# Second FFN: eight chunks done whole as four pairs, the first weight tiles of a pair with seven block products

## The chip, the cores and the metric

The kernel runs on one core of a Trainium2 chip. The metric is device time in microseconds (us), as the median of several runs. Engines are named as in the profile: PE is TensorE (matrix products), PEld its loading of the stationary operand, DVE is VectorE, ACT is ScalarE, POOL is GpSimd, SP is SyncE, which issues the DMAs.

## The reference

The kernel computes one block on 256 tokens of width 2048, in float32: a first gated feed-forward layer (FFN), a mixer (differential attention on half of the width, a causal depthwise convolution on the other), and a second FFN, each with a residual sum. Each of the three is entered through an RMS norm whose result is scaled and shifted, and left through a gate; scales, shifts and gates come from a vector c.

```python
ada = silu(c) @ w_ada + b_ada                  # 9 vectors of 2048: shift, scale, gate, three times
h = rms_norm(x) * (1 + scale) + shift
x = x + 0.5 * gate * swiglu(h, w_gu, w_down)   # FFN, first and last
...
def swiglu(h, w_gu, w_down):                   # d_ff = 5632
    g, u = split(h @ w_gu)
    return (silu(g) * u) @ w_down
```

## The kernel before

**Precision.** TensorE multiplies in a reduced-width float32 (fp32r). So each operand is split in a high part (a cast on ScalarE) and a low part (the difference, on VectorE), and a product is three matmuls: high by high, high by low, low by high (`mm3`, lines 331, 335 and 336). The activations are the stationary operand (128 x 128), the weights the moving one (128 x 512).

**Weights.** `w_tile` (from line 290) loads a weight tile of 512 x 512 numbers (1 MB) through SyncE's queue into one of four buffers (`raw`), and splits it in two halves of 128 x 1024 per engine instruction: `whi` by ScalarE (line 307), `wlo` by VectorE (line 309). There are four buffers of each, so the halves are at most four at a time, one of them under TensorE. `mm_tile` (line 344) runs the 24 matmuls of a tile: four k, two halves of the tokens, three matmuls each, into two PSUM banks, and then a `tick`, which starts what was put off by some tiles with `after_tiles`. Six PSUM banks are in the pool `acc`, two in `tp`.

**Order.** A planner (the framework's) orders each engine's instructions ahead of time: by the order of the program text, by when operands and buffers come free in its own estimate of the times. On the chip each engine runs its list in order and waits at semaphores.

**The feed-forward layer** (`ffn`, line 664). The 11264 columns of w_gu are 22 chunks of 512 (256 gate columns, 256 up columns); the 2048 rows are four tiles (pc 0 to 3). For the second FFN:

1. The first stage (`stage_a`, line 686): for every chunk the product with the first tile (pc 0) alone, copied by ScalarE from the banks into a part buffer of the chunk (line 691). The rest of the normed activations is made meanwhile (`pieces`), as soon as its scales and shifts are there.
2. Chunks begun early (`early`, here 3, 4 and 5): the product with tile pc 1 is added to the part (line 811).
3. The main groups (line 892): chunks 0 to 2 together, then one chunk at a time, over the tiles that are left. `finish` (line 852) of a chunk comes after the first tile of the next: VectorE adds the banks to the part (855), ScalarE takes silu of the gate half (856), VectorE multiplies (857). The result is then transposed: it is a 4-byte number in two 2-byte planes (copy by ScalarE, 861), turned by a DMA transpose from SyncE's queue (876), put together again (ScalarE, 870) and split in high and low (352, 353). In the second FFN all chunks go this way, in the first FFN the odd ones; the even ones are transposed on TensorE (886).
4. The down projection (`down_strassen`, line 490): 22 tiles in each of two halves; seven of the 22 are done as a 2 x 2 block product with seven block products (Strassen's method in Winograd's form) in place of eight; the others plainly.

**Modulation rows.** `ada(j)` (line 189) computes 128 of the 9 x 2048 modulation numbers: a 1 MB DMA into a `raw` buffer and one multiply-and-sum against the broadcast c (`c_bc`) on VectorE (line 195), and for every second j an addition of the bias (199). There are 144; those of the second FFN are rows 96 to 143. They are dealt out among the weight tiles by shares: in the second FFN 0.6 a tile until row 128, and then 0.5 until row 144. `modulation` (line 230) forms 1 + scale, times the norm's weight, one k at a time (line 237).

**Buffers.** 28 buffers of 4 KB per partition (`blk`) hold the parts, the normed activations (eight) and the transposed results; six (`tmp`) of 2 KB hold temporaries. `c_bc` has one buffer of its own, which the down projection uses again once the rows are done.

## Time and profile before

| | |
|---|---|
| median of 3 runs | 1821.1 us (1820.06 to 1821.19) |
| the profiled execution | 1820.38 us, of which the span of the profile 1818.5 us |
| TensorE | busy 1790.5 us, 8033 matmuls |
| weight load (PEld) | busy 1475.1 us |
| VectorE | busy 1521.1 us |
| ScalarE | busy 1056.5 us |
| GpSimd | busy 29.2 us |
| DMA | 507.19 MB, mean 279 GB/s |

The span runs from the first instruction to the last. The busy time of an engine is the time in which at least one of its instructions runs. Matmuls overlap: each is shown with some 390 ns, though they start closer together, so what one takes is read from successive starts. The same holds for VectorE and ScalarE to a smaller extent. A group's row names the line, the engine, the operation, what is written and read, the count, the busy time and the mean duration in ns, and the engine's idle time before it with what ended that.

### The profile page before, as it was taken

To read this page: it belongs to the slowest core of one execution; us is meant where nothing else is said; L and a number is where in the kernel's file an instruction comes from. 1 tells how busy PE (TensorE), PEld (TensorE's weight loads), DVE (VectorE), ACT (ScalarE), POOL (GpSimd) and SP (SyncE) were. 2 spreads that over 40 slices of the span, in tenths; PEclk is the share of its full clock that TensorE was granted. 3 is DMA by queue.
4 is the path that set the end of the run, shared out by engine and by line. 5 is a ranking of instruction groups with operands and counts; after the bars stand their busy time and mean duration, and the time that the engine had idled before them with its cause. 6 is when DMAs were issued, how large, how long until landed. Compare 5 with 4: busy or idle time off the path is not lost.

```text
span 1818.5 us, 21751 instructions
## 1 busy us (share of the span) xinstructions
PE 1790.5 (98%) x8033; PEld 1475.1 (81%) x8033; DVE 1521.1 (84%) x2018; ACT 1056.5 (58%) x1563; POOL 29.2 (2%) x29
## 2 busy tenths in 40 slices
...
GB/s 378 357 307 313 354 338 295 351 318 331 334 339 373 331 335 344 275 257 205 182 143 163 175 330 276 324 329 313 281 304 310 316 222 205 212 199 219 199 216 107
DMA packets 118138, 507.19 MB, mean 279 GB/s; under 512 B 53600, under 2 KB 54032, under 8 KB 60560
## 3 DMA queue, kind: packets, MB, share of 16 engines
...
## 4 chain that ended last, share of the span: by engine, by line
PE 86%; DVE 8%; ACT 2%; DMA 2%; issue 2%; SPq 0%; POOLq 0%; POOL 0%; DVEq 0%; ACTq 0%
PE acc L335 27%; PE acc L336 27%; PE acc L331 27%; DVE wlo L309 2%; DVE raw L195 1%; PE tp L335 1%; ACT whi L307 1%; PE tp L336 1%; PE tp L331 1%; DMA blk<-in_w_gu_dram 1%; PE acc L1171 1%; DVE wlo L538 1%; DVE blk L1063 1%; DMA raw<-in_w_gu_dram 0%; DVE blk L309 0%
## 5 line engine op out<-in xcount | busy, mean ns | idle before, releaser
L335 PE MATMUL acc<-wlo,blk 128*128 128x512 f32 x2340 | 913.0, 390 | 8.4 <-DVE wlo L309 8.4
L331 PE MATMUL acc<-whi,blk 128*128 128x512 f32 x2343 | 910.3, 391 | 2.5 <-ACT blk L405 1.3
L336 PE MATMUL acc<-whi,blk 128*128 128x512 f32 x2340 | 912.0, 390 | 0.0
L309 DVE TENSOR_TENSOR wlo<-raw,whi 128x1024 fp32r<-128x1024 f32 (+1 forms) x581 | 692.5, 1211 | 187.8 <-ACT whi L307 186.8
L307 ACT CAST whi<-raw 128x1024 fp32r<-128x1024 f32 (+1 forms) x581 | 597.2, 1044 | 428.8 <-PE acc L336 285.7
L335 PEld LDWEIGHTS acc<-wlo,blk 128*128 128x128 f32 x2340 | 439.5, 188 | 103.9 <-DVE wlo L309 13.4
L331 PEld LDWEIGHTS acc<-whi,blk 128*128 128x128 f32 x2343 | 440.0, 188 | 94.5 <-ACT whi L307 2.0
L336 PEld LDWEIGHTS acc<-whi,blk 128*128 128x128 f32 x2340 | 439.3, 188 | 92.0 <-DVE blk L407 0.8
L195 DVE CUSTOM_DVE_ANT_0 raw<-raw,c_bc 128x2048 f32<-128x2048 f32 x142 | 324.2, 2285 | 4.9 <-DMA raw<-in_w_ada_dram 4.9
L537 ACT CAST whi<-raw 128x1024 fp32r<-128x1024 f32 (+1 forms) x56 | 53.0, 946 | 68.2 <-PE tp L336 31.9
L538 DVE TENSOR_TENSOR wlo<-raw,whi 128x1024 fp32r<-128x1024 f32 (+1 forms) x56 | 60.8, 1088 | 19.3 <-ACT whi L537 19.1
L1063 DVE SCALAR_TENSOR_TENSOR blk<-blk,cst,blk 128x247 f32<-128x247 f32 (+21 forms) x176 | 70.5, 460 | 0.0
L870 ACT COPY tmp<-tmp 128x1024 uint16<-128x1024 uint16 x33 | 44.9, 1359 | 37.7 <-DMA tmp<-tmp 37.6
L691 ACT COPY blk<-acc 128x512 f32<-128x512 f32 x72 | 41.6, 588 | 42.7 <-PE acc L336 40.7
L856 ACT ACTIVATE blk<-blk 128x256 f32<-128x256 f32 x88 | 34.9, 413 | 43.7 <-DVE blk L855 43.5
L855 DVE TENSOR_TENSOR blk<-acc,blk 128x512 f32<-128x512 f32 x88 | 57.2, 683 | 2.1 <-PE acc L336 2.1
L331 PE MATMUL acc<-blk,blk 128*128 128x512 f32 x104 | 40.7, 394 | 0.9 <-ACT blk L323 0.9
L861 ACT COPY tmp<-blk 128x1024 uint16<-128x1024 uint16 x33 | 34.4, 1043 | 10.4 <-DVE blk L857 10.2
L335 PE MATMUL acc<-blk,blk 128*128 128x512 f32 x100 | 39.1, 391 | 0.5 <-DVE blk L309 0.5
L336 PE MATMUL acc<-blk,blk 128*128 128x512 f32 x100 | 39.1, 392 | 0.0
L857 DVE TENSOR_TENSOR blk<-blk 128x256 f32<-128x256 f32 x88 | 34.9, 418 | 0.7 <-ACT blk L856 0.6
L353 DVE TENSOR_TENSOR blk<-tmp,blk 128x512 fp32r<-128x512 f32 x33 | 22.7, 688 | 14.4 <-ACT blk L352 14.4
...
## 6 DMA issues: line engine op xcount, KB each, us to landing
raw<-in_w_gu_dram SPq DMA_DIRECT2D x161, 1024.0 KB, 6.4
...
```

Source lines behind the costliest of these rows:

```text
L195: nc.vector.tensor_tensor_reduce(out=raw, in0=raw, in1=c_bc, scale=1.0, scalar=0.0, op0=ALU.mult, op1=ALU.add, accum_out=ada_cols[g][:, j ...
L307: nc.scalar.copy(out=hi[:, :m, :], in_=rw)
L309: nc.vector.tensor_sub(out=lo[:, :m, :], in0=rw, in1=hi[:, :m, :].bitcast(F32))
L331: nc.tensor.matmul(acc, ah, wh, start=start, stop=False)
L335: nc.tensor.matmul(acc, ah, wl, start=False, stop=False)
L336: return nc.tensor.matmul(acc, al, wh, start=False, stop=stop)
L537: nc.scalar.copy(out=hi[:, :n, :], in_=src)
L538: nc.vector.tensor_sub(out=lo[:, :n, :], in0=src, in1=hi[:, :n, :].bitcast(F32))
L691: last_part[0] = nc.scalar.copy(out=parts[c][:, t, :], in_=accs[t])
L855: nc.vector.tensor_add(out=p[:, t, :], in0=accs[t], in1=p[:, t, :])
L870: nc.scalar.copy(out=src.bitcast(U16).rearrange("p i t (s b) -> p b t i s", b=2), in_=turned)
L1063: nc.vector.scalar_tensor_tensor(out=y[:, d:], in0=u, scalar=w, in1=y[:, d:], op0=ALU.mult, op1=ALU.add)
```

## The change

In the second FFN the last eight chunks (14 to 21) are no longer done in the first stage. They are done whole, as four pairs, after chunk 12; chunk 13 comes last. Each pair begins with `pair_first`: the first weight tiles of both its chunks are taken as one 2 x 2 block matrix (two blocks of rows, two chunks), and the activations as another (two halves of the tokens, two blocks of k), and the product is formed with seven block products. Four PSUM banks are used; the partial sums that go to more than one result are copied out by ScalarE as they come (`kept`, four temporaries for a pair), and are added when the chunks are finished. The other three tiles of each chunk follow into the same four banks. The sums of the activations are formed once, ahead of chunk 12 (`pair_sums`), in the buffer of `c_bc`; so all modulation rows are asked for ahead of it.

With this, the early chunks become 3 to 9, and the shares become 0.72 and 0.8 rows a tile. In both FFNs `finish` uses the chunk's own buffer for the planes and for what the DMA turned, with one temporary for the product, and the second FFN's copy back is put off by a tile. From row 32 on the biases are added eight at a time, and for the mixer and the second FFN the scales are formed four at a time.

```diff
--- before.py
+++ after.py
@@ -59,6 +59,7 @@
 KEPT = 6
 CROSSBAR = {0: range(1, NCH, 2), 96: range(NCH)}
 TURNED_BY_PE = ((0, 1), (48, 1), (48, 2), (48, 3))
+WHOLE = {0: 0, 96: 8}
 RMS_EPS = 1e-6
 LN_EPS = 1e-5
 LAM_INIT = 0.8 - 0.6 * float(np.exp(-0.3 * 0))
@@ -194,9 +195,10 @@
         nc.sync.dma_start(out=raw, in_=w_ada[j])
         nc.vector.tensor_tensor_reduce(out=raw, in0=raw, in1=c_bc, scale=1.0, scalar=0.0, op0=ALU.mult,
                                        op1=ALU.add, accum_out=ada_cols[g][:, j % 8:j % 8 + 1])
-        if j % 2 == 1:
-            p0, o = _COLS["bada"][0] + j - 1, j % 8 - 1
-            nc.vector.tensor_add(out=ada_cols[g][:, o:o + 2], in0=ada_cols[g][:, o:o + 2], in1=cst[:, p0:p0 + 2])
+        n = 2 if j < 32 else 8
+        if j % n == n - 1:
+            p0, o = _COLS["bada"][0] + j + 1 - n, (j + 1 - n) % 8
+            nc.vector.tensor_add(out=ada_cols[g][:, o:o + n], in0=ada_cols[g][:, o:o + n], in1=cst[:, p0:p0 + n])
 
     ada_next = [2]
     credit = [0.0]
@@ -229,7 +231,16 @@
 
     def modulation(base, k, norm):
 
-        if (base, k) not in mods:
+        if (base, k) not in mods and base > 0:
+            ada_until(base + 2 * k // 8 * 8 + 8)
+            a = ada_cols[(base + 2 * k) // 8]
+            k0 = k // 4 * 4
+            G = scales[:, base // 3 + k0:base // 3 + k0 + 4]
+            nc.vector.scalar_tensor_tensor(out=G, in0=a[:, 0:8:2], scalar=1.0, in1=col(norm)[:, k0:k0 + 4],
+                                           op0=ALU.add, op1=ALU.mult)
+            for i in range(4):
+                mods[base, k0 + i] = (G[:, i:i + 1], a[:, 2 * i + 1:2 * i + 2])
+        elif (base, k) not in mods:
             j = base + 2 * k
             ada_until(j + 2)
             a = ada_cols[j // 8]
...
@@ -661,6 +673,71 @@
                 else:
                     evac_last(2 + n, plain[i], t, gbc[2 + n])
 
+    def pair_sums(st):
+
+        res = []
+        keep = cbp.tile([P, 2, 2, 4, P], F32R, tag="c_bc", name="sums")
+        for j in range(2):
+            full = tmp([P, 2, S])
+            nc.vector.tensor_add(out=full, in0=st.hh[0][:, j:4:2].bitcast(F32), in1=st.hl[0][:, j:4:2].bitcast(F32))
+            a11, a21, a12, a22 = full[:, 0, :P], full[:, 0, P:], full[:, 1, :P], full[:, 1, P:]
+            q = tmp([P, 4, P])
+            nc.vector.tensor_add(out=q[:, 0], in0=a21, in1=a22)
+            nc.vector.tensor_sub(out=q[:, 1], in0=q[:, 0], in1=a11)
+            nc.vector.tensor_sub(out=q[:, 2], in0=a11, in1=a21)
+            nc.vector.tensor_sub(out=q[:, 3], in0=a12, in1=q[:, 1])
+            hi, lo = keep[:, 0, j], keep[:, 1, j]
+            nc.scalar.copy(out=hi, in_=q)
+            nc.vector.tensor_sub(out=lo, in0=q, in1=hi.bitcast(F32))
+            res.append([(hi[:, i], lo[:, i]) for i in range(4)])
+        return res
+
+    def pair_first(w_gu, c, act, sums, banks):
+
+        raws = []
+        for n in range(2):
+            raw = rawp.tile([P, 4, 512], F32, tag="raw", name=nm("raw"))
+            w_dma[0] = nc.sync.dma_start(out=raw, in_=w_gu[c + n, 0].rearrange("p (k n) -> p k n", k=4))
+            raws += [raw[:, 0:2, :], raw[:, 2:4, :]]
+        b11, b21, b12, b22 = raws
+        c11, c21, c12, c22 = banks
+
+        def split(src):
+            hi = whp.tile([P, 2, 512], F32R, tag="whi", name=nm("whi"))
+            lo = wlp.tile([P, 2, 512], F32R, tag="wlo", name=nm("wlo"))
+            nc.scalar.copy(out=hi, in_=src)
+            nc.vector.tensor_sub(out=lo, in0=src, in1=hi.bitcast(F32))
+            return hi, lo
+
+        def times(acc, a, w, start=False):
+            for j in range(2):
+                mm3(acc, a(j), (w[0][:, j, :], w[1][:, j, :]), start and j == 0, j == 1, more=not start)
+
+        def kept(acc):
+            u = tmp([P, 512])
+            nc.scalar.copy(out=u, in_=acc)
+            return u
+
+        t2 = blk([P, 2, 512])
+        nc.vector.tensor_sub(out=b12, in0=b12, in1=b11)
+        nc.vector.tensor_sub(out=t2, in0=b22, in1=b12)
+        times(c22, lambda j: act(j, 0), split(b11), True)
+        u11 = kept(c22)
+        nc.vector.tensor_sub(out=b11, in0=t2, in1=b11)
+        times(c12, lambda j: sums[j][0], split(b12), True)
+        u22 = kept(c12)
+        times(c22, lambda j: sums[j][1], split(t2))
+        u12 = kept(c22)
+        nc.vector.tensor_sub(out=t2, in0=b21, in1=t2)
+        times(c21, lambda j: act(2 + j, 1), split(t2), True)
+        times(c11, lambda j: act(2 + j, 0), split(b21), True)
+        times(c22, lambda j: sums[j][2], split(b11))
+        u21 = kept(c22)
+        times(c12, lambda j: sums[j][3], split(b22))
+        tick()
+        tick()
+        return u11, u21, u12, u22
+
     def ffn(st, w_gu, w_dn, gate_base, ada_a, ada_b, nxt, again, early, early_3):
 
 
@@ -682,6 +759,7 @@
 
         parts = [None] * NCH
         last_part = [None]
+        whole = NCH - WHOLE[base]
 
         def stage_a(c, w, accs, ts, n=4):
             mm_tile(accs, w, act, 0, True, True, ts, (0, n))
@@ -795,7 +873,7 @@
                     stage_a(c, w, accs, (t,))
             with tc.issue_after(st.last.ins):
                 ada_a_share(12)
-            for c in range(3, NCH):
+            for c in range(3, whole):
                 w = w_tile(w_gu[c, 0])
                 stage_a(c, w, [acc_tile() for _ in range(NT)], (0, 1))
                 ada_a_share(4)
@@ -849,49 +927,46 @@
 
         aT = [None] * NCH
 
-        def finish(c, accs):
-            p = parts[c]
+        def finish(c, accs, us=None):
+            p = parts[c] or blk([P, NT, 512])
+            m = tmp([P, NT, 256]) if c in CROSSBAR[base] else p[:, :, 256:]
             for t in range(NT):
-                nc.vector.tensor_add(out=p[:, t, :], in0=accs[t], in1=p[:, t, :])
+                nc.vector.tensor_add(out=p[:, t, :], in0=accs[t], in1=us[t] if us else p[:, t, :])
                 nc.scalar.activation(out=p[:, t, :256], in_=p[:, t, :256], func=AF.Silu)
-                nc.vector.tensor_mul(out=p[:, t, 256:], in0=p[:, t, :256], in1=p[:, t, 256:])
-
+                nc.vector.tensor_mul(out=m[:, t, :], in0=p[:, t, :256], in1=p[:, t, 256:])
             if c in CROSSBAR[base]:
-                planes = tmp([P, 2, NT, 256], U16)
-                nc.scalar.copy(out=planes, in_=p[:, :, 256:].bitcast(U16).rearrange("p t (f b) -> p b t f", b=2))
-
-            def split(src):
+                planes, turned = p[:, 0, :].bitcast(U16), p[:, 1, :].bitcast(U16)
+                nc.scalar.copy(out=planes.rearrange("p (b f) -> p b f", b=2),
+                               in_=m.rearrange("p t f -> p (t f)").bitcast(U16).rearrange("p (f b) -> p b f", b=2))
+
+            def rest():
+                if c in CROSSBAR[base]:
+                    nc.sync.dma_start_transpose(out=turned.rearrange("p (j s) -> p j s", s=P), in_=planes)
+                    after_tiles(1, joined)
+                    return
+                tp = tp_tile((P, 2, S))
+                for t in range(NT):
+                    for i in range(2):
+                        nc.tensor.transpose(tp[:, i, t * P:(t + 1) * P], m[:, t, i * P:(i + 1) * P], ident)
+                halves(tp)
+
+            def joined():
+                src = p[:, 0, :].rearrange("p (i t s) -> p i t s", i=2, t=NT)
+                nc.scalar.copy(out=src.bitcast(U16).rearrange("p i t (s b) -> p b t i s", b=2),
+                               in_=turned.rearrange("p (b t i s) -> p b t i s", b=2, t=NT, i=2))
+                halves(src.rearrange("p i t s -> p i (t s)"))
+
+            def halves(src):
                 a = blk([P, 2, 2, S], F32R)
                 split_from_psum(src, a[:, 0], a[:, 1])
                 aT[c] = a
 
-            def joined(turned):
-                src = tmp([P, 2, NT, P])
-                nc.scalar.copy(out=src.bitcast(U16).rearrange("p i t (s b) -> p b t i s", b=2), in_=turned)
-                split(src.rearrange("p i t s -> p i (t s)"))
-
-            def rest():
-                if c in CROSSBAR[base]:
-                    turned = tmp([P, 2, NT, 2, P], U16)
-                    nc.sync.dma_start_transpose(out=turned.rearrange("p b t i s -> p (b t i) s"),
-                                                in_=planes.rearrange("p b t f -> p (b t f)"))
-                    if base == 0:
-                        after_tiles(1, lambda: joined(turned))
-                    else:
-                        joined(turned)
-                    return
-                src = tp_tile((P, 2, S))
-                for t in range(NT):
-                    for i in range(2):
-                        nc.tensor.transpose(src[:, i, t * P:(t + 1) * P],
-                                            p[:, t, 256 + i * P:256 + (i + 1) * P], ident)
-                split(src)
-
             after_tiles(1, rest)
 
-        groups = [[0, 1, 2]] + [[c] for c in range(3, NCH)]
+        groups = [[0, 1, 2]] + [[c] for c in range(3, whole)]
         pend = []
-        for g in groups:
+
+        def run(g):
             accs = {c: [acc_tile() for _ in range(NT)] for c in g}
             for i, (pc, ks) in enumerate(segments(g[0], start_of[g[0]], 4)):
                 ada_until(base + 8 * pc + 8)
@@ -910,6 +985,28 @@
                             finish(*pend.pop(0))
             for c in g:
                 pend.append((c, accs[c]))
+
+        last = groups.pop() if whole < NCH else None
+        sums = None
+        for g in groups:
+            if last and g is groups[-1]:
+                ada_until(144)
+                sums = pair_sums(st)
+            run(g)
+        if last:
+            for i, c in enumerate(range(whole, NCH, 2)):
+                banks = [acc_tile() for _ in range(4)] if i % 2 == 0 else \
+                    [acc_tile(), acc_tile(), tp_tile(), tp_tile()]
+                us = pair_first(w_gu, c, act, sums, banks)
+                while pend:
+                    finish(*pend.pop(0))
+                for pc in range(1, 4):
+                    for n in range(2):
+                        w = w_tile(w_gu[c + n, pc])
+                        mm_tile(banks[2 * n:2 * n + 2], w, act, 4 * pc, False, pc == 3, more=True)
+                for n in range(2):
+                    pend.append((c + n, banks[2 * n:2 * n + 2], us[2 * n:2 * n + 2]))
+            run(last)
 
         def a_act(k, t):
             a = aT[k // 2]
@@ -1426,7 +1523,7 @@
         norm2.piece(0, t, True)
 
 
-    ffn(norm2, w_gu2, w_dn2, 128, (0.6, 128), (0.5, 144), None, [], [[3], [4], [5]], [])
+    ffn(norm2, w_gu2, w_dn2, 128, (0.72, 128), (0.8, 144), None, [], [[c] for c in range(3, 10)], [])
 
 
 def _f(a):
```

13 lines of the change are left out of this document (7 added, 6 removed).

## The prediction

> **What bounds the kernel now.** I read the page's first part, then the busy time by stretches, then the timelines of the engines inside the second FFN.
>
> ```profile
> span 1818.5 us, 21751 instructions
> PE 1790.5 (98%) x8033; PEld 1475.1 (81%) x8033; DVE 1521.1 (84%) x2018; ACT 1056.5 (58%) x1563; POOL 29.2 (2%) x29
> GB/s 378 357 307 313 354 338 295 351 318 331 334 339 373 331 335 344 275 257 205 182 143 163 175 330 276 324 329 313 281 304 310 316 222 205 212 199 219 199 216 107
> ```
>
> TensorE is busy 98% of the span. So the count of matmuls sets the time, and a gap on TensorE adds to it.
>
> Stretches next (start:end, length, busy us of PE, PEld, DVE, ACT, POOL with counts, clock, DMA share, GB/s). The first is the first FFN's main groups. The others are the second FFN: first weight tiles of all 22 chunks; chunks begun early and chunks 0 to 2; groups 3 onwards while modulation rows still load; groups after the last row; the down projection in three parts.
>
> ```profile
> 363.00:546.00 183.00, 179.78 (x800) 147.13 (x799) 163.25 (x233) 95.78 (x117) 0.00 (x0) 1.00 0.87 331
> ...
> 1104.70:1222.00 117.30, 117.13 (x520) 96.76 (x519) 92.51 (x109) 83.62 (x115) 1.47 (x1) 1.00 0.92 323
> 1222.00:1271.00 49.00, 49.00 (x217) 40.34 (x215) 37.83 (x46) 27.30 (x32) 0.00 (x0) 1.00 0.95 327
> 1271.00:1335.00 64.00, 64.00 (x283) 52.89 (x283) 53.01 (x65) 44.53 (x54) 0.00 (x0) 1.00 0.84 278
> 1335.00:1455.00 120.00, 120.00 (x531) 99.36 (x530) 98.79 (x116) 73.44 (x83) 0.00 (x0) 1.00 0.89 313
> 1455.00:1591.00 136.00, 136.00 (x601) 112.61 (x600) 79.37 (x90) 79.05 (x91) 0.00 (x0) 1.00 0.66 212
> 1591.00:1637.00 46.00, 45.21 (x197) 36.34 (x196) 45.72 (x68) 26.52 (x32) 0.00 (x0) 1.00 0.53 199
> 1637.00:1773.00 136.00, 136.00 (x601) 112.61 (x601) 114.27 (x129) 70.25 (x74) 0.00 (x0) 1.00 0.57 212
> ```
>
> In the second FFN up to 1591 TensorE loses 0.2 us in all. So no wait is there to be won: the change can gain by its matmuls only, and whatever it delays is a new loss. The clock is 1.00 throughout. The first FFN's main groups lose 183.00 - 179.78 = 3.2 us with VectorE at 89% and DMA at 331 GB/s. This is the nearest row for what the change makes of the second FFN's groups.
>
> What a matmul costs is its spacing, not its duration (they overlap). First and last of 57 successive 512-column matmuls:
>
> ```profile
> 1329.67 0.39 PE L331 MATMUL acc<-whi,blk 128*128 128x512 f32 x1
> ...
> 1342.36 0.39 PE L336 MATMUL acc<-whi,blk 128*128 128x512 f32 x1
> ```
>
> (1342.36 - 1329.67) / 56 = 0.2266 us. A weight tile (24 matmuls) is 5.44 us, and half of it, the unit in which weights are split, 2.72 us.
>
> **The matmuls removed.** The first tiles of two chunks are 2 chunks x 2 token halves x 4 k x 3 = 48 matmuls. Seven block products of 2 k x 3 are 42, or 9.52 us in place of 10.88. Four pairs save 24 matmuls x 0.2266 = **5.44 us**. No other TensorE work is added or dropped.
>
> **VectorE and ScalarE work added.** Their prices, start to start, from VectorE's timeline, then ScalarE's:
>
> ```profile
> 1304.82 2.28 DVE L195 CUSTOM_DVE_ANT_0 raw<-raw,c_bc 128x2048 f32<-128x2048 f32 x1
> 1307.03 0.08 DVE L195 DVE_READ_ACCUMULATOR2_ANT ada<- 128x1 f32 x1
> 1307.03 1.22 DVE L309 TENSOR_TENSOR wlo<-raw,whi 128x1024 fp32r<-128x1024 f32 x1
> 1308.17 0.68 DVE L353 TENSOR_TENSOR blk<-tmp,blk 128x512 fp32r<-128x512 f32 x1
> 1308.77 1.22 DVE L309 TENSOR_TENSOR wlo<-raw,whi 128x1024 fp32r<-128x1024 f32 x1
> 1309.90 1.28 DVE L855 TENSOR_TENSOR blk<-acc,blk 128x512 f32<-128x512 f32 x2
> 1311.10 0.41 DVE L857 TENSOR_TENSOR blk<-blk 128x256 f32<-128x256 f32 x1
> 1311.44 1.22 DVE L309 TENSOR_TENSOR wlo<-raw,whi 128x1024 fp32r<-128x1024 f32 x1
> ```
>
> ```profile
> 1278.87 1.06 ACT L307 CAST whi<-raw 128x1024 fp32r<-128x1024 f32 x1 [1.04 <-PE acc L336]
> 1279.83 1.04 ACT L861 COPY tmp<-blk 128x1024 uint16<-128x1024 uint16 x1
> ```
>
> VectorE takes 1.14 us for 1024 columns, 0.60 for 512, 0.34 for 256, 2.21 for a modulation row. ScalarE takes 0.96 for a cast. Finishing a chunk is 2 x 0.60 + 2 x 0.34 + 0.60 = 2.48 us of VectorE.
>
> A pair's seven products need 4 differences and 7 low halves: 11 x 1.14 = 12.5 us of VectorE in 9.52 us of TensorE. The whole pair has 12 more low halves (13.7) and two finishes (5.0): 31.2 us in 9.52 + 6 x 5.44 = 42.2 us, so 74%. On average it hides, under the six plain tiles. Locally it must come out of the lead. The four split buffers let VectorE be three halves ahead. That is 8.2 us in plain tiles, but only 3 x 1.36 = 4.1 us where a half lasts one product.
>
> The nearest rows are the seven-product chunks of the down projection, which already work so. Its first two, with their sums, need still more VectorE (the 46 us stretch: 45.72 busy), and TensorE waited twice:
>
> ```profile
> 1601.59 0.50 PE L335 MATMUL tp<-wlo,in_c_bc 128*128 128x512 f32 x1 [0.53 <-DVE wlo L538]
> ...
> 1612.66 0.73 PE L331 MATMUL acc<-whi,blk 128*128 128x512 f32 x2 [0.21 <-ACT whi L307]
> ```
>
> That is 0.74 us for two; the later ones up to 1773 lost nothing (136.00 of 136.00). Bounds for the four pairs: 0, and 12.5 - 9.52 = 3.0 us for each with no lead, 12. I take the dearer chunks' 0.37 each: **+1.5 us**. The sixteen copies out of the banks replace sixteen of the first-tile stage. The activation sums (two of: one 512-column add, four of 128, one low half) stand ahead of chunk 12, beside three plain tiles that need 6.9 of 16.3 us: nothing, or 2 x 1.9 = 3.8 us if that cover is gone.
>
> **The modulation rows, squeezed.** Rows 109 to 143 must be reduced before the sums take the buffer of c. By the code's shares they had 22 + 3 + 9 + 32 = 66 tiles; now they have 14 + 7 + 9 + 20 = 50, since eight chunks leave the first stage. The shares go from 0.6 and 0.5 rows a tile to 0.72 and 0.8. Chunks 3 to 9 come with two tiles each and a finish: 4 x 1.14 + 1.6 x 2.21 + 2.48 = 10.6 us of VectorE in 10.88, 97%, behind three finishes at once (7.4 us) at chunk 3. DMA: a tile per 5.44 us is 193 GB/s, with 0.8 rows 347. What a crossbar transpose takes is read from two stretches of equal traffic, 0.66 against 0.57 share, with this count in the first:
>
> ```profile
> tmp<-tmp SPq DMA_TRANSPOSE x9, 3.5
> ```
>
> (0.66 - 0.57) x 136 / 9 = 1.4 us of all sixteen engines. So by the 331 GB/s at 0.87 share the new demand is 0.91 + 1.4 / 10.88 = 1.04: just full for 14 tiles. Bounds: 0 (lead of 8.2 us covers it), or 0.04 x 76 = 3.0 us of DMA plus the 4.6 us by which chunk 3's first two tiles overrun on VectorE (4 x 1.14 + 3.5 + 7.4 - 10.88), 7.6. I take the first FFN's rate, 3.2 us in 183, for the 20 tiles (109 us) with 0.8: **+1.9 us**. The nearest row speaks for it: VectorE 89%, DMA 0.87. The four more chunks begun early add 8 adds of 0.60, at 2.28 + 1.6 + 1.2 = 5.1 of 5.44 us a tile: nothing, or 4.8 us if they cannot hide.
>
> The Trainium skill, "DMA: Bandwidth & Descriptors", section "Where 436 GB/s comes from", gives about 358 GB/s as a core's share of HBM. That speaks against these rates: 347 would leave 3%. The slices of 373 and 378 GB/s stand above it, so the measurement decides; by the page the squeeze would be nearer its upper bound and the sum about zero.
>
> **The small edits, and the first FFN.** Bias adds go from one per two rows to one per eight, scales from one per k to one per four:
>
> ```profile
> L199 DVE TENSOR_TENSOR ada<-ada,cst x71: 149/160/164, 29.8 to 1453.6; 128x2 f32<-128x2 f32 x71
> ...
> L237 DVE SCALAR_TENSOR_TENSOR scales<-ada,cst x47: 150/159/161, 30.0 to 1259.9; 128x1 f32<-128x1 f32 x47
> ```
>
> 42 and 24 fewer, 10.5 us of VectorE over the whole kernel, mostly where TensorE does not wait. The crossbar path now uses the chunk's own buffer and one temporary in place of three, and the second FFN's copy back waits a tile longer. That unblocks ScalarE's queue, which waited for the transposes:
>
> ```profile
> ACT tmp L870 <- DMA tmp<-tmp: 37.6, 25, 3.5
> ```
>
> Against it, in the first FFN 22 part buffers and 6 of activations fill all 28, and an odd chunk now holds its own until the result has one; it waits for an even chunk to free one. Bounds: -3.2 us (its idle goes) to +3.2 (it doubles). I take **0**.
>
> **The sum.** -5.44 + 1.5 + 1.9 = -2.0 us. The profiled execution took 1820.38 us (span 1818.5 and 1.9 around it): 1818.3. The median of the runs stands 0.7 above it, 1821.1, so 1819.0.
>
> **Rivals.** (1) All hidden: 1821.1 - 5.4 = **1815.7**. For it: idle of zero now, 74% over a pair, lead in every stretch. Against: both engines that feed TensorE are near full in chunks 3 to 9.
> (2) The squeeze is not covered: its upper bound 7.6 in place of 1.9 gives -5.44 + 1.5 + 7.6 = +3.7, **1824.8**; half of it, 1821.0. For: 1.04 share. Against: slices of 373 GB/s without idle in the first FFN's down projection, 181 us from 546:
>
> ```profile
> 546.00:727.00 181.00, 181.00 (x800) 149.91 (x799) 145.39 (x149) 76.16 (x81) 0.00 (x0) 1.00 0.91 345
> ```
>
> (3) The slower one: the temporaries. A pair keeps four copies until it is finished, in the next pair, which wants four more; there are six. So the third copy (u12) waits for the finish's first two adds on VectorE, and the sixth product, which goes on in the same bank, waits for that copy. If those adds stand behind the pair's remaining work (one difference, four low halves, two of the next tile: 7 x 1.14 = 8.0 us after the pair's start), the copy ends at 8.0 + 1.2 + 0.6 = 9.8 us, where the sixth product was due at 5 x 1.36 = 6.8. That is 3.0 us in three pairs, 9.0 in place of three of the 0.37: -5.44 + 9.0 + 0.4 + 1.9 = +5.9, **1827.0**; it decides from 2.2 us a pair on. Against: VectorE waits for split buffers in between and has 6.8 - 4 x 1.14 = 2.2 us free before the sixth product, where 1.2 is wanted.
> The Trainium skill, "PSUM — Partial Sum Buffer", section "Engine vs sequencer instructions", has VectorE's queue as strict first in, first out: by that, what stands behind cannot pass.
> (4) The first FFN gains from its freed temporaries, to -2 or more beside full hiding: below 1814.
>
> **How the numbers follow.** My sum with its own neighbourhood (1816.9 to 1820.5) 0.41; all hidden 0.27; squeeze 0.15; temporaries 0.12; first FFN 0.05. About 0.2%, 3.6 us, is what a measurement can tell from no change: 1817.5 and 1824.7. Faster: 0.27 + 0.05 + 0.06 of my own case = 0.38. Slower: 0.12 + 0.04 of the squeeze = 0.16. The rest, 0.46, is within. The range 1814.8 to 1825.2 leaves out the first FFN's case and most of the temporaries'.
>
> **What would show it.** TensorE records should fall by about 24. In the stretch of the pairs, idle ahead of the third product's or a later matmul with a low half as releaser would be the 0.37 term; a wait of the sixth product for a copy out of a bank, in pairs two to four alone, would be the temporaries. DMA share at 1.0 and low halves late in chunks 3 to 9 would be the squeeze; TensorE at full there and a span near 1813 would be rival 1. I am wrong in kind if the loss lies before 1100.

## The result and the profile after

The changed kernel takes **1833.0 us** (median; 1830.5 to 1834.5) against 1821.0 before: a ratio of 1.0064, 95% interval 1.0051 to 1.0077. It is slower by 0.64%, 12.0 us. Forecast was 1819.0, with a range that ended at 1825.2.

The first part of the page after and its GB/s by slices (the execution took 1830.5 us, the fastest of the six, so 2.5 of the 12.0 us are not in this trace):

```profile
span 1828.7 us, 21709 instructions
...
PE 1790.2 (98%) x8009; PEld 1469.0 (80%) x8009; DVE 1553.0 (85%) x2000; ACT 1065.8 (58%) x1577; POOL 29.2 (2%) x29
...
GB/s 377 358 310 312 349 330 325 330 326 313 344 337 366 336 339 334 276 253 186 183 161 149 175 346 269 323 352 282 348 350 237 203 215 239 218 206 212 202 213 109
```

TensorE has 8009 records in place of 8033: the 24 matmuls are gone as forecast. Yet the span is 10.2 us longer, so TensorE waits some 15 us more. Where, is read from the busy time by stretches (start:end, length, busy us of PE, PEld, DVE, ACT and POOL with counts, clock, DMA share, GB/s). The first is in the first FFN; then the second FFN's first stage with most of the early chunks; the main groups; the stretch before the pairs (chunks 10 to 12); the start of the first pair; the pairs.

```profile
546.00:727.00 181.00, 179.33 (x791) 147.85 (x790) 143.87 (x136) 75.01 (x81) 0.00 (x0) 1.00 0.91 346
1105.00:1222.00 117.00, 113.29 (x497) 92.51 (x497) 99.57 (x113) 77.86 (x102) 1.48 (x1) 1.00 0.87 323
1222.00:1345.00 123.00, 123.00 (x545) 101.79 (x544) 108.95 (x130) 79.17 (x94) 0.00 (x0) 1.00 0.95 322
1345.00:1402.00 57.00, 52.80 (x226) 41.54 (x225) 49.70 (x63) 34.69 (x40) 0.00 (x0) 1.00 0.89 329
1402.00:1444.00 42.00, 39.93 (x175) 32.48 (x174) 30.27 (x30) 24.36 (x28) 0.00 (x0) 1.00 0.60 207
1444.00:1600.00 156.00, 156.00 (x686) 128.12 (x686) 112.10 (x120) 101.94 (x122) 0.00 (x0) 1.00 0.64 211
```

The row of before for 1345 to 1402:

```profile
1345.00:1402.00 57.00, 57.00 (x254) 47.18 (x253) 45.88 (x54) 34.56 (x39) 0.00 (x0) 1.00 0.93 328
```

Before, TensorE had been idle for 0.2 us from 1104.7 to 1591. Now it is idle for 3.7 us in the first stage, 4.2 just before the pairs and 2.1 at the first pair. The clock is 1.00 in all of these. The mean rate hardly differs between the two kernels from 1345 to 1402 (328 and 329 GB/s), and yet one of them loses nothing there.

A busy time hides part of each wait, since matmuls overlap. So I also went through TensorE's timeline from start to start, and took what a distance between two starts exceeds 0.2266 us (one 512-column matmul). The large ones:

```profile
1193.40 0.50 PE L346 MATMUL acc<-wlo,blk 128*128 128x512 f32 x1 [1.46 <-DVE wlo L320]
...
1216.92 0.50 PE L346 MATMUL acc<-wlo,blk 128*128 128x512 f32 x1 [1.47 <-DVE wlo L320]
...
1383.03 0.39 PE L347 MATMUL acc<-whi,blk 128*128 128x512 f32 x1
1384.95 0.73 PE L342 MATMUL acc<-whi,blk 128*128 128x512 f32 x2 [1.53 <-ACT whi L318]
1386.37 0.50 PE L346 MATMUL acc<-wlo,blk 128*128 128x512 f32 x1 [0.69 <-DVE wlo L320]
...
1408.23 0.49 PE L342 MATMUL acc<-whi,blk 128*128 128x512 f32 x1 [1.62 <-ACT whi L708]
1409.18 0.49 PE L342 MATMUL acc<-whi,blk 128*128 128x512 f32 x1 [0.45 <-ACT whi L708]
```

The bracket is the idle time and its releaser. 1383.03 to 1384.95 is 1.92 us, of which 1.69 is lost. Summed over each stretch ("lost" below always means this sum, in us):

| stretch | 363–546 | 546–727 | 727–1100 | 1100–1222 | 1222–1345 | 1345–1402 | 1402–1444 | 1444–1600 |
|---|---|---|---|---|---|---|---|---|
| before | 6.3 | 0.1 | 8.1 | 1.6 | 0.3 | 0.0 | 0.0 | 0.1 |
| after | 4.8 | 2.3 | 9.1 | 5.4 | 0.1 | 6.2 | 2.7 | 0.8 |

From 1100 to 1600 that is 15.2 against 2.0: 13.2 us more lost for 5.4 us of matmuls saved, so 7.8 of the span's 10.2 us. The first FFN and the mixer have 1.7 more (the mixer, 727 to 1100, also has shorter matmuls, so the count misses short waits there).

The rows are not dense where most is lost. VectorE's sums of rows that start from 1105 to 1222, 1222 to 1345 and 1345 to 1402 are 15, 10 and 6 before, and 16, 14 and 5 after. The stretch that loses 6.2 us has one row fewer than before, and the stretch with four more loses 0.1. So a loss can show later than where the rows were added.

What feeds these waits is seen one engine further back. Waits of ScalarE's casts for a weight tile's DMA from 1105 to 1402 (total us, times, longest), before and then after:

```profile
ACT whi L307 <- DMA raw<-in_w_gu_dram: 1.4, 2, 0.7
```

```profile
ACT whi L318 <- DMA raw<-in_w_gu_dram: 36.0, 19, 4.3
```

Weights come late 19 times where they came late twice. The end of the first stage shows how that reaches TensorE: ScalarE after, and VectorE after.

```profile
1210.93 2.00 ACT L318 CAST whi<-raw 128x1024 fp32r<-128x1024 f32 x2 [3.95 <-DMA raw<-in_w_gu_dram]
```

```profile
1211.58 2.28 DVE L196 CUSTOM_DVE_ANT_0 raw<-raw,c_bc 128x2048 f32<-128x2048 f32 x1
...
1214.36 1.37 DVE L889 TENSOR_TENSOR blk<-acc,blk 128x512 f32<-128x512 f32 x2 [0.49 <-PE acc L347]
1215.65 3.49 DVE L320 TENSOR_TENSOR wlo<-raw,whi 128x1024 fp32r<-128x1024 f32 x3
```

These are the tiles with which chunks 3 to 9 are begun early (1181 to 1223 after the change). The casts wait 3.95 us for a tile. VectorE, meanwhile, has started a modulation row and then the adds of an early chunk, so the low half that TensorE wants begins at 1215.65, and TensorE goes on at 1216.92.

### The profile page after: what moved, and what is told of

It is laid out like the page before. It is cut to its first block, busy times and chain, and to the rows that moved or that the text cites. A ratio compares the mean times of both kernels' runs of the same rounds, so it can differ in the third digit from the quotient of the medians.

```text
span 1828.7 us, 21709 instructions
## 1 busy us (share of the span) xinstructions
PE 1790.2 (98%) x8009; PEld 1469.0 (80%) x8009; DVE 1553.0 (85%) x2000; ACT 1065.8 (58%) x1577; POOL 29.2 (2%) x29
## 3 DMA queue, kind: packets, MB, share of 16 engines
HBM read 492.37 MB, written 2.12 MB: 270 GB/s over the span
## 5 line engine op out<-in xcount | busy, mean ns | idle before, releaser
L342 PE MATMUL acc<-whi,blk 128*128 128x512 f32 x2251 | 873.5, 392 | 7.3 <-ACT whi L318 3.6
L347 PE MATMUL acc<-whi,blk 128*128 128x512 f32 x2248 | 876.2, 390 | 0.1
L318 ACT CAST whi<-raw 128x1024 fp32r<-128x1024 f32 x565 | 578.0, 1044 | 408.2 <-PE acc L347 223.6
L320 DVE TENSOR_TENSOR wlo<-raw,whi 128x1024 fp32r<-128x1024 f32 x565 | 670.2, 1211 | 151.8 <-ACT whi L318 150.8
L342 PEld LDWEIGHTS acc<-whi,blk 128*128 128x128 f32 x2251 | 422.3, 188 | 98.2 <-ACT whi L318 6.5
L347 PEld LDWEIGHTS acc<-whi,blk 128*128 128x128 f32 x2248 | 422.0, 188 | 88.0 <-DVE blk L419 0.8
L549 ACT CAST whi<-raw 128x1024 fp32r<-128x1024 f32 (+1 forms) x56 | 53.0, 947 | 69.0 <-PE tp L347 31.9
L550 DVE TENSOR_TENSOR wlo<-raw,whi 128x1024 fp32r<-128x1024 f32 (+1 forms) x56 | 60.9, 1089 | 19.2 <-ACT whi L549 18.9
L955 ACT COPY blk<-blk 128x1024 uint16<-128x1024 uint16 x33 | 44.5, 1360 | 24.1 <-DMA blk<-blk 23.9
L342 PE MATMUL tp<-whi,blk 128*128 128x512 f32 x127 | 49.4, 389 | 0.0
L346 PE MATMUL tp<-wlo,blk 128*128 128x512 f32 x127 | 49.4, 389 | 0.0
L347 PE MATMUL tp<-whi,blk 128*128 128x512 f32 x127 | 49.4, 389 | 0.0
L342 PE MATMUL acc<-blk,blk 128*128 128x512 f32 x104 | 40.7, 394 | 0.9 <-ACT blk L334 0.9
L347 PE MATMUL acc<-blk,blk 128*128 128x512 f32 x100 | 39.4, 394 | 0.6 <-DVE blk L491 0.6
```

Of the source, the lines that this page charges most:

```text
L318: nc.scalar.copy(out=hi[:, :m, :], in_=rw)
L320: nc.vector.tensor_sub(out=lo[:, :m, :], in0=rw, in1=hi[:, :m, :].bitcast(F32))
L342: nc.tensor.matmul(acc, ah, wh, start=start, stop=False, skip_group_check=more)
L346: nc.tensor.matmul(acc, ah, wl, start=False, stop=False, skip_group_check=more)
L347: return nc.tensor.matmul(acc, al, wh, start=False, stop=stop, skip_group_check=more)
L549: nc.scalar.copy(out=hi[:, :n, :], in_=src)
```

## The experiments

Each is told against the kernel before, run beside it on the same chip (medians of before: 1820.6 to 1821.9 us). A short diff shows the edit; "changed" is the changed kernel.

### Which part of the change: rates, rows, pairs, small edits

**rates_alone** is the kernel before with the new shares and early chunks, and nothing else.

```diff
-    ffn(norm2, w_gu2, w_dn2, 128, (0.6, 128), (0.5, 144), None, [], [[3], [4], [5]], [])
+    ffn(norm2, w_gu2, w_dn2, 128, (0.72, 128), (0.8, 144), None, [], [[c] for c in range(3, 10)], [])
```

> The kernel before with one thing of the change alone: the early chunks 3 to 9 and the shares 0.72 and 0.8 rows a tile. No pairs, no other edit; same matmuls as before. Squeeze theory (too many modulation rows in too few tiles starve TensorE in the second FFN): TensorE loses 5 to 10 us between 1105 and 1400, with low halves late; 1826 to 1831 us. Rival, the pairs themselves: nothing lost, 1821. Rival, the small edits: 1821.

Measured: 1830.4 us, 1.0052 [1.0037, 1.0067]. Its stretches before the first pair's place:

```profile
1105.00:1222.00 117.00, 115.88 (x507) 94.08 (x506) 94.90 (x114) 81.91 (x115) 1.47 (x1) 1.00 0.87 325
...
1345.00:1402.00 57.00, 54.10 (x234) 43.19 (x233) 51.62 (x65) 37.24 (x45) 0.00 (x0) 1.00 0.89 325
1402.00:1444.00 42.00, 41.03 (x180) 32.96 (x179) 31.29 (x37) 24.48 (x28) 0.00 (x0) 1.00 0.92 333
```

Without any pair it loses 3.0, 4.4 and 1.9 us there (and 1.1 from 1222 to 1345): most of the loss comes with the new shares and early chunks, not with the pairs. This run does not separate the two; four_pairs_mix, below, has the early chunks without the dense shares.

**no_gate_rows** is the changed kernel without rows 128 to 143 (the last gate is taken from other rows).

```diff
+        base = min(base, 112)
...
-                ada_until(144)
+                ada_until(128)
...
-    ffn(norm2, w_gu2, w_dn2, 128, (0.72, 128), (0.8, 144), None, [], [[c] for c in range(3, 10)], [])
+    ffn(norm2, w_gu2, w_dn2, 128, (0.72, 128), (0.8, 128), None, [], [[c] for c in range(3, 10)], [])
```

> The changed kernel, with the 16 rows of the second FFN's gate (128 to 143) left out of the computation: neither loaded nor summed (the gate is then formed of rows 112 to 127). Four pairs as in the change. Squeeze theory: the 6.2 us lost between 1345 and 1402 fall to under 1, the 2.7 lost in the first pair (a backlog) to under 1, and the 3.6 of the first stage stay: 1824 to 1826 us. Rival, the pairs themselves: the first pair still loses 2 to 3 us and 6 us stay ahead of it, 1831 to 1833.

Measured: 1825.2 us, 1.0028 [1.0017, 1.0039].

```profile
1105.00:1222.00 117.00, 113.79 (x501) 92.99 (x500) 99.64 (x114) 77.72 (x102) 1.48 (x1) 1.00 0.90 327
...
1345.00:1402.00 57.00, 56.34 (x248) 46.13 (x247) 42.61 (x56) 36.73 (x45) 0.00 (x0) 1.00 0.58 186
1402.00:1444.00 42.00, 42.00 (x185) 34.47 (x184) 30.96 (x30) 24.94 (x30) 0.00 (x0) 1.00 0.60 207
```

Where the rows are gone so is the loss: 6.2 becomes 1.0, nearly all of it the first pair's start, which falls in this row here, and the 2.7 of the next row becomes 0.3. The first stage, which keeps its 0.72, still loses 5.3. The activation sums and the four pairs are all there, and in this trace they cost little (1.0, 0.3 and 0.7). It is of the fastest of the ten executions, 1821.7 us; what makes the median 3.5 us longer is not seen in it.

**small_edits** is the changed kernel with no pair and with the shares and early chunks of before.

```diff
-WHOLE = {0: 0, 96: 8}
+WHOLE = {0: 0, 96: 0}
...
+    ffn(norm2, w_gu2, w_dn2, 128, (0.6, 128), (0.5, 144), None, [], [[3], [4], [5]], [])
```

> The changed kernel without pairs (all 22 chunks as before) and with the shares and early chunks of before: what is left of the change are the biases by eight, the scales by four, and the finish in the chunk's own buffer with the copy back put off by a tile. If the 2.2 us by which the second FFN begins later come of these edits: 1823 us, with the same two stalls at 549 and 778 us. If they come of the pairs through the planner: 1821. Squeeze: nothing lost in the second FFN either way.

Measured: 1827.2 us, 1.0037 [1.0024, 1.0051]. It loses nothing from 1222 to 1444, but at the end of the groups:

```profile
1589.76 0.79 PE L346 MATMUL acc<-wlo,blk 128*128 128x512 f32 x1 [4.65 <-DVE wlo L320]
```

A finished chunk now stays in its own buffer until it is split, and splitting takes one more. With 22 parts and eight buffers of activations none is free, so the splits of 16 chunks pile up until the groups end, in front of this low half: 9.7 us of VectorE in one piece, from 1578.86. In the changed kernel eight chunks have no part in the first stage, and this wait does not occur. So this run tells of the small edits without pairs only.

**three_pairs**: three pairs, and rows spread more thinly.

```diff
-WHOLE = {0: 0, 96: 8}
+WHOLE = {0: 0, 96: 6}
...
+    ffn(norm2, w_gu2, w_dn2, 128, (0.66, 128), (0.54, 144), None, [], [[c] for c in range(3, 9)], [])
```

> The changed kernel with three pairs (chunks 16 to 21) in place of four, early chunks 3 to 8, shares 0.66 and 0.54, which are enough for it: 18 matmuls saved, 4.1 us. Squeeze theory: it is nearly gone, the second FFN loses 1 to 3 us, with the 2.2 us ahead of it 1820 to 1822 us. Rival, the pairs themselves: three quarters of the loss stays, about 1829.

Measured: 1820.6 us, 0.9997 [0.9986, 1.0008]: the same as before. From 1100 to 1600 it loses some 4.6 us, about 2.5 more than before, for 4.1 saved.

### What it is in the rows: VectorE's sums, the bytes, the bookkeeping

**rows_short_sum**: the changed kernel; rows 109 to 143 are loaded whole, but only 256 of 2048 columns are summed.

```diff
+        e = 256 if j >= 109 else D
+        nc.vector.tensor_tensor_reduce(out=raw[:, :e], in0=raw[:, :e], in1=c_bc[:, :e], scale=1.0, scalar=0.0, op0=ALU.mult,
...
```

> The changed kernel with the modulation rows of the second FFN (109 to 143) loaded in full, but each summed over 256 of its 2048 columns only (the rest of the sum is left out): the same DMA, 0.35 us of VectorE a row in place of 2.29. If the squeeze is one of VectorE: the 3.6 us of the first stage, the 6.2 between 1345 and 1402 and the first pair's 2.7 nearly all go, 1821 to 1823 us. If it is one of the DMA or of SyncE's queue: they stay, 1831 to 1833.

Measured: 1832.1 us, 1.0060 [1.0044, 1.0076].

```profile
1105.00:1222.00 117.00, 114.62 (x504) 93.91 (x505) 72.18 (x116) 78.57 (x102) 1.47 (x1) 1.00 0.88 327
```

VectorE falls from 99.6 to 72.2 us in the first stage, from 85% to 62%, and nothing is won. The time of VectorE's sums is not the cause.

**rows_short_load**: the opposite. 256 columns of each of these rows are loaded, and VectorE sums 2048 columns of another tensor.

```diff
+        if j >= 109:
+            nc.sync.dma_start(out=raw[:, :256], in_=w_ada[j][:, :256])
+            nc.vector.tensor_tensor_reduce(out=raw, in0=c_bc, in1=c_bc, scale=1.0, scalar=0.0, op0=ALU.mult,
...
```

> The changed kernel with the same rows loaded to 256 of 2048 columns only (128 KB in place of 1 MB), while VectorE sums 2048 columns as before, of another tensor: same VectorE, an eighth of the rows' DMA. If the squeeze is one of the DMA: the losses of the second FFN nearly all go, 1821 to 1823 us. If it is one of VectorE: they stay, 1831 to 1833. If both have to be short for it to go, each of these two runs keeps a part.

Measured: 1822.8 us, 1.0005 [0.9996, 1.0015].

```profile
1105.00:1222.00 117.00, 116.38 (x514) 95.50 (x513) 103.73 (x119) 81.26 (x106) 1.47 (x1) 1.00 0.69 226
...
1345.00:1402.00 57.00, 53.69 (x230) 43.02 (x229) 49.17 (x64) 34.27 (x43) 0.00 (x0) 0.98 0.68 220
```

VectorE is as busy as in the changed kernel and as many transfers are issued, yet 10 us are back. The first stage loses 1.6 as before. What is left in the second row (5.3 us lost) is mostly the first pair's start, which falls in this window here as the kernel is earlier:

```profile
1399.49 0.50 PE L347 MATMUL acc<-whi,sums 128*128 128x512 f32 x1 [2.12 <-ACT tmp L723]
```

A low half that is late costs 0.9, this wait for the copy of the first product out of its bank 2.3, and the matmuls behind it, which run at about half their pace into the next row, 1.7. This trace is of the slowest of its ten executions, 1824.7 us. So it is the transfers' size that counts: **the rows' DMA bytes are a necessary part of the loss.**

**row_edits** is before with the biases added eight rows at a time and the scales formed four at a time.

```diff
+        n = 2 if j < 32 else 8
+        if j % n == n - 1:
...
```

> The kernel before with the row edits alone: biases by eight from row 32 on, scales by four for the mixer and the second FFN. If the two waits at 549 us come of these: about 1 to 2 us slower than before, 1822.5. If they come of the finish in the chunk's own buffer: 1820.5 to 1821.5, with no wait there.

Measured: 1822.2 us, 1.0005 [0.9996, 1.0015]: no change.

**old_finish_1**: the changed kernel, with the first FFN's finish as before (three temporaries).

```diff
+        if base == 0:
+            def finish(c, accs):
+                p = parts[c]
...
```

> The changed kernel with the first FFN's finish as before (three temporaries; the second FFN's stays in the chunk's own buffer). If that edit makes the two waits at 549 us: they go, about 2 us less than the changed kernel, 1831. If not: 1833 with the waits there. The losses of the second FFN stay either way.

Measured: 1832.5 us, 1.0059 [1.0044, 1.0074], against 1.0064 with the new one: no difference to be told. Lost in the first FFN: 6.9 and 0.1 us, where the changed kernel has 4.8 and 2.3.

### Where the rows' traffic could go

**rows_pool_queue**: the changed kernel; rows 109 onwards are issued from GpSimd's queue, so that no weight stands behind a row in SyncE's.

```diff
+        (nc.gpsimd if j >= 109 else nc.sync).dma_start(out=raw, in_=w_ada[j])
```

> The changed kernel with the DMAs of rows 109 to 143 issued from GpSimd's queue in place of SyncE's; all else alike, the same bytes. If the rows starve the weights by standing ahead of them in SyncE's queue (waiting there for a buffer): most of the 12 us lost in the second FFN goes, 1822 to 1825 us. If it is the transfers themselves, or the four buffers that rows and weights share: 1830 to 1834.

Measured: 1861.6 us, 1.0216 [1.0192, 1.0239]: far worse. VectorE's and ScalarE's waits for DMA from 1105 to 1402 (VectorE's for rows are 2.4 before, and not seen after):

```profile
DVE raw L196 <- DMA raw<-in_w_ada_dram: 26.8, 13, 3.4
```

```profile
ACT whi L318 <- DMA raw<-in_w_gu_dram: 23.5, 12, 3.3
```

The casts' wait falls from 36.0 to 23.5, but now VectorE stands still for rows, with the weights' low halves behind it.

**rows_in_blk**: the changed kernel; these rows go, in halves, into buffers of the pool of 28 in place of the four that the weights use.

```diff
+                wa = blk([P, 1024])
...
+                nc.sync.dma_start(out=wa, in_=w_ada[j, :, hs])
...
```

> The changed kernel with rows 109 to 143 loaded, in two halves of 512 KB each, into buffers of the 28 in place of the four that the weights use; two sums of 1024 columns and one small addition in place of one sum of 2048. Same bytes, same queue. If it is the four shared buffers that make weights late: most of the loss goes, 1822 to 1825 us. If it is the transfers' time or the queue: 1830 to 1834.

Measured: 1834.1 us, 1.0074 [1.0060, 1.0088]. Rows in other buffers win nothing, so the four shared buffers are hardly it (the halves also bring more, smaller transfers and sums).

**four_pairs_mix**: the changed kernel with four rows more in the mixer, and 0.62 rows a tile throughout.

```diff
-            if ci == 1 or ci == 0 and pc > 1:
-                ada_share(1.0, 104)
+            if 0 < ci < 4 or ci == 0 and pc > 1:
+                ada_share(1.0, 108)
...
+    ffn(norm2, w_gu2, w_dn2, 128, (0.62, 144), (0.62, 144), None, [], [[c] for c in range(3, 10)], [])
```

> The changed kernel with four more rows done in the mixer (DMA share 0.4 to 0.7 there), so that the second FFN begins with row 113, and one share of 0.62 rows a tile throughout it, near the 0.6 of before, which lost nothing. Four pairs. If density of rows is the whole of it: the first stage loses under 1 us, 1345 to 1402 under 2, the pairs 1 to 2; -5.4 + 2 to 4, 1818 to 1820 us. If the pairs themselves cost: above 1823.

Measured: 1826.1 us, 1.0029 [1.0018, 1.0039]. From 1100 to 1600 it loses 5.2 us in place of 15.2: with fewer rows the four pairs do gain there (5.2 - 2.0 - 5.4 is -2.2 against before). The early chunks are as in the changed kernel, and from 1100 to 1402 it loses 3.9 us where that loses 11.7. But the mixer (727 to 1100) pays where the rows were added, here and then before:

```profile
815.00:850.00 35.00, 30.25 (x131) 23.24 (x130) 34.76 (x57) 19.56 (x33) 0.00 (x0) 1.00 0.68 255
```

```profile
815.00:850.00 35.00, 35.00 (x159) 28.95 (x158) 31.91 (x49) 23.02 (x37) 0.00 (x0) 1.00 0.59 211
```

The DMA engines are at 0.68 there, but VectorE goes from 91% to 99%, and TensorE waits for low halves; 8.7 us more are lost in the mixer. So these four rows found no free place there; others were not tried.

**two_pairs**: two pairs with the shares of before.

```diff
-WHOLE = {0: 0, 96: 8}
+WHOLE = {0: 0, 96: 4}
...
+    ffn(norm2, w_gu2, w_dn2, 128, (0.6, 128), (0.5, 144), None, [], [[3], [4], [5]], [])
```

> The changed kernel with two pairs (chunks 18 to 21), and early chunks and shares exactly as before (0.6 and 0.5). 12 matmuls saved, 2.7 us. If density of rows is the whole of it: nothing lost in the first stage and the groups, the pairs 0.5 to 1.5, so 1.2 to 2.2 us less than before, 1819 to 1820. If the pairs themselves cost what was lost in the changed kernel: 1824 or more.

Measured: 1826.9 us, 1.0033 [1.0020, 1.0045].

```profile
1253.70 0.79 PE L342 MATMUL acc<-whi,blk 128*128 128x512 f32 x1 [3.56 <-ACT blk L490]
```

This is the shares' fault: with 18 chunks in the first stage 0.6 does not bring the last rows of the scales in time, and the normed activations that need them are late. The matmuls behind this wait run at half their pace for 5 us, which costs 2.9 us more.

### How the loss depends on the bytes, and fewer pairs again

**rows_half_load**: as rows_short_load, with 1024 columns loaded.

```diff
+            nc.sync.dma_start(out=raw[:, :1024], in_=w_ada[j][:, :1024])
...
```

> The changed kernel with rows 109 to 143 loaded by half: 1024 of their 2048 columns, while VectorE still sums 2048 columns for each (of another tensor, so the modulation of the second FFN isn't the reference's). With the full load the time was 1833.0 us, with an eighth of it 1822.8. Theory 1, the loss goes with the bytes: half of the bytes is 4/7 of the way from an eighth up to the whole lost less, so 1822.8 + 10.2 x 3/7 = 1827.2 us, 1826 to 1828.5. Theory 2, a threshold (the loss comes only when demand passes what the DMA engines can give: 193 GB/s of weights plus 0.8 rows a tile is 347 GB/s with the whole, 270 with half): nothing lost at half, 1822 to 1824. Theory 3, it is the number of transfers and not their size: 1832 or more.

Measured: 1829.6 us, 1.0040 [1.0027, 1.0053]. Nothing lost (1.0005) and everything lost (1.0064) both lie outside; 1.0030, in proportion, is inside, though the time is a microsecond above what theory 1 allowed. A threshold between 270 and 347 GB/s as the only cause is excluded. But the trace is not a tidy half. In the first stage it loses 5.0 us, nearly as much as the whole load, and there VectorE waits for a row while the low halves stand behind it:

```profile
1189.01 2.29 DVE L197 CUSTOM_DVE_ANT_0 raw<-c_bc 128x2048 f32<-128x2048 f32 x1 [4.37 <-DMA raw<-in_w_ada_dram]
```

**three_pairs_only** is before with the three pairs of three_pairs (0.68 rows a tile in the first stage), and the first FFN's finish and the rows' bookkeeping as before; the second FFN's finish is that of the changed kernel.

```diff
...
-    ffn(norm2, w_gu2, w_dn2, 128, (0.6, 128), (0.5, 144), None, [], [[3], [4], [5]], [])
+    ffn(norm2, w_gu2, w_dn2, 128, (0.68, 128), (0.54, 144), None, [], [[c] for c in range(3, 9)], [])
```

> The kernel before with three pairs alone (chunks 16 to 21; chunks 3 to 8 begun early; shares of 0.68 rows a tile in the first stage and 0.54 behind), the first FFN's finish and the rows' bias and scale edits left as before. Three pairs save 18 matmuls, 4.1 us. The same three pairs with all other edits ran at 1820.55, the same as before. Theory 1, the other edits cost some 1 to 2 us (the rows' edits alone measured 1822.2 against 1820.9): 1818.0 to 1819.5. Theory 2, three pairs' own loss is what gives the 4.1 us back: 1820.0 to 1821.5.

Measured: 1823.9 us, 1.0014 [1.0004, 1.0023]. Both theories are missed, and the first has its sign wrong: the other edits do not cost anything that leaving them out gives back. At its first pair it loses 3.3 us, where three_pairs lost 1.1.

**two_pairs_more**: two_pairs with denser rows.

```diff
-    ffn(norm2, w_gu2, w_dn2, 128, (0.6, 128), (0.5, 144), None, [], [[3], [4], [5]], [])
+    ffn(norm2, w_gu2, w_dn2, 128, (0.7, 128), (0.52, 144), None, [], [[3], [4], [5]], [])
```

> The changed kernel with two pairs (chunks 18 to 21; chunks 3 to 5 begun early), and shares of 0.7 rows a tile in the first stage and 0.52 behind, in place of the 0.6 and 0.5 with which two pairs ran at 1826.9 and TensorE waited 3.7 us for row 128. Two pairs save 12 matmuls, 2.7 us. Theory 1, the wait was the shares' alone: it is gone, and the time is 1819.0 to 1821.5. Theory 2, denser rows in the first stage cost what the wait did (with 0.72 in the first stage the weights came late by some 3.6 us): 1822.5 to 1825.

Measured: 1821.9 us, 1.0001 [0.9993, 1.0010]. Theory 1 holds for the wait: it is gone. The 2.7 us of matmuls are given back once more: 4.6 us are lost from 1100 to 1600, 2.6 more than before.

Across the runs in which SyncE loads the rows whole, the loss up to 1222 follows the share: 1.6 us at 0.6 and 0.66 rows a tile, 1.8 at 0.68, 3.1 at 0.7, 3.0 to 5.4 at 0.72 (7.5 with the rows in halves).

### The order in SyncE's queue

SyncE issues all these transfers in order, and a crossbar transpose of a finished chunk stands in it until its planes are ready. How long SyncE stood ahead of these transposes from 1222 to 1402 (what it waited for: total us, times, longest), before and then after:

```profile
SPq L876 <- ACT whi L307: 7.9, 4, 2.9
SPq L876 <- ACT blk L352: 5.3, 2, 3.3
SPq L876 <- ACT tmp L861: 2.4, 2, 1.4
```

```profile
SPq L944 <- ACT whi L318: 37.1, 6, 8.0
SPq L944 <- ACT blk L939: 31.4, 5, 7.5
SPq L944 <- ACT blk L935: 5.5, 1, 5.5
```

That is 74 us in place of 16. What goes with it is in the GB/s by slices of 1.4 us from 1345 to 1402, before and then after:

```profile
GB/s 298 328 414 397 247 293 420 356 379 167 402 314 209 351 431 431 253 402 213 98 299 356 323 368 414 397 196 305 397 368 333 218 402 289 154 414 414 431 224 431
```

```profile
GB/s 139 322 425 420 420 437 420 414 61 221 230 425 402 420 448 420 420 408 420 29 33 208 247 443 408 431 420 431 420 420 420 213 368 173 117 394 345 443 305 29
```

After, the DMA engines run at 400 to 450 GB/s for up to 11 us and then stand nearly empty (61, 29, 33) while SyncE waits. A mean share of 0.89 hides both. But 56 of the 74 us lie from 1222 to 1345, where 0.1 us is lost, and in four_pairs_mix SyncE stands for 78 us and TensorE loses 2.7 from 1222 to 1402. So the pauses alone do not make the loss.

**turns_later**: the changed kernel; such a transpose is issued one weight tile later.

```diff
-            after_tiles(1, rest)
+            after_tiles(2 if base else 1, rest)
```

> The changed kernel with one edit: in the second FFN the crossbar transpose of a finished chunk is issued after two further weight tiles and not after one, so one more weight tile stands ahead of it in SyncE's queue. In the changed kernel SyncE stands still ahead of these transposes for 55.8 us in the stretch from 1222 to 1345 and 18.2 in 1345 to 1402 (before: 11.2 and 4.4), and the weights and rows behind them are issued late. Theory 1, the order in SyncE's queue makes the loss of 6.2 us in 1345 to 1402 and part of the backlog at the first pair: 1824 to 1828 us, with TensorE's loss there under 2. Theory 2, the bytes of the rows alone make it, in whatever order: 1831 to 1834. Neither touches the 3.8 us of the first stage, where no such transpose stands in the queue.

Measured: 1829.6 us, 1.0049 [1.0036, 1.0062]. SyncE's waits ahead of the transposes from 1222 to 1402 fell from 74 to 55 us, and most of the first pair's loss is gone:

```profile
SPq L944 <- ACT whi L318: 44.4, 8, 7.4
SPq L944 <- ACT blk L939: 5.8, 3, 3.2
SPq L944 <- ACT blk L935: 4.6, 1, 4.6
```

```profile
1345.00:1402.00 57.00, 52.97 (x230) 42.60 (x229) 51.10 (x65) 32.84 (x38) 0.00 (x0) 1.00 0.88 324
1402.00:1444.00 42.00, 42.00 (x186) 34.33 (x185) 31.64 (x32) 25.23 (x30) 0.00 (x0) 1.00 0.58 207
```

Lost: 5.2 us in place of 6.2, and 0.4 in place of 2.7. In the stretch that theory 1 named, SyncE still stands for 15.8 us (18.2 without the edit), so the run hardly puts the theory to the test there. At the pair ScalarE's list has another order in this run (see the pairs' own cost, below), so it is not shown that the queue made the difference. In time the intervals of the two kernels overlap; 3.5 us is likely, not shown.

**turns_act**: the changed kernel, with these transposes issued from ScalarE's queue.

```diff
-                    nc.sync.dma_start_transpose(out=turned.rearrange("p (j s) -> p j s", s=P), in_=planes)
+                    (nc.scalar if base else nc.sync).dma_start_transpose(out=turned.rearrange("p (j s) -> p j s", s=P), in_=planes)
```

> The changed kernel with one edit: the second FFN's crossbar transposes are issued from ScalarE's queue in place of SyncE's, so nothing of them stands ahead of a weight tile or a row. Theory 1 (the order in SyncE's queue): 1824 to 1828 us where ScalarE's issue time, 1.24 us each on SyncE now, hides in its idle 40%. Theory 2 (the bytes alone): 1831 to 1835. A third: ScalarE's issues, 22 x 1.24 = 27 us, delay the casts of weights and cost more than they save: over 1835.

Measured: 1921.0 us, 1.0540 [1.0524, 1.0555]. The third case, but not by the issues' 27 us: ScalarE waits for the transposes to land (1105 to 1700), and casts of weights stand behind.

```profile
ACT blk L955 <- DMA blk<-blk: 107.6, 18, 15.1
```

**three_pairs_later**: three_pairs with the edit of turns_later.

```diff
-            after_tiles(1, rest)
+            after_tiles(2 if base else 1, rest)
```

> The kernel with three pairs (chunks 16 to 21; 0.66 and 0.54 rows a tile; chunks 3 to 8 begun early), which ran at 1820.55, the same as before, with the same edit as in the run above it: transposes after two further tiles. It lost 2.2 us in the two waits ahead of 1100 and 1.1 at its first pair. Theory 1 (queue order): 1818.5 to 1820. Theory 2: 1820 to 1822, no change.

Measured: 1823.4 us, 1.0019 [1.0009, 1.0028], slower than three_pairs without it. Here too the first pair loses (1.9 us, in a profiled execution of 1827.5 us), so later transposes are no general remedy.

## Why the prediction was wrong, point by point

**The matmuls removed** (-5.44): right. 24 records fewer, and four_pairs_mix gains in the second FFN once there are fewer rows.

**The pairs' own cost** (+1.5, bounds 0 and 12): inside the bounds, but the mechanism was another. I priced VectorE's differences and low halves. What the traces show is ScalarE's list, in which the copies out of the banks stand ahead of casts that TensorE needs; I had taken these copies to cost nothing, as they "replace sixteen of the first-tile stage". At the first pair of the changed kernel the cast of the fourth product's matrix (line 708) stands behind the copy of the third product (718), which can start only when that product is done:

```profile
1406.65 0.59 ACT L718 COPY tmp<-acc 128x512 f32<-128x512 f32 x1 [0.46 <-PE acc L347]
1407.13 1.05 ACT L708 CAST whi<-blk 128x1024 fp32r<-128x1024 f32 x1
```

So TensorE waits 2.1 us there by the order of the list, and it is not shown that lateness from further back adds to it. At the second pair, and in turns_later and no_gate_rows at the first, that cast stands behind the copy of the first product. The other three pairs lose 0.8 us in all; the four together lose some 2 us without the gate rows and 1.2 with later transposes. But the first pair costs 3.3 us in three_pairs_only and 4.9 in rows_short_load. So 1.5 us was about right for some of these lists and too little for others.

**The activation sums ahead of chunk 12** ("nothing, or 3.8", taken as nothing): in the changed kernel the two waits at 1384.95 and 1386.37, 2.7 us with the slower starts behind them, are theirs in part. ScalarE's list there:

```profile
1379.74 0.62 ACT L364 CAST blk<-blk 128x512 fp32r<-128x512 f32 x1
1383.33 0.62 ACT L690 CAST sums<-tmp 128x512 fp32r<-128x512 f32 x1 [2.97 <-DVE ada L196]
1383.85 1.04 ACT L318 CAST whi<-raw 128x1024 fp32r<-128x1024 f32 x1
```

The cast of the sums waits for VectorE, which does one of the last rows first, and the weights' cast stands behind it. But that weight tile, issued at 1375.45, had landed only at 1383.06 by its semaphore, 0.2 us before TensorE ran out of work. So perhaps half of the 2.7 us is the sums' (an estimate: the cast started 0.8 us after the landing, and the sums' low half took 0.6 us of VectorE ahead of the weights'), and the rest a late tile. My cover for the sums, 6.9 of 16.3 us, left out the rows and the finish that stand in the same lists. Without the last rows it is nothing (no_gate_rows).

**The modulation rows, squeezed** (+1.9, bounds 0 and 7.6): **this is the step that failed.** The rates with the early chunks alone cost 8.5 us of TensorE (10.4 lost from 1100 to 1444 in rates_alone, 1.9 before) and 9.3 in the time, above my upper bound. In the changed kernel 3.8 us more than before are lost up to 1222, and 6.2 from 1345 to 1402, of which the sums have a part. Three things in the working were wrong:

- I priced it by the first FFN's row (3.2 us lost in 183 at 331 GB/s), as if the same rate and share meant the same loss. The same 323 GB/s at 0.92 of before lost 0.2 us, and 323 at 0.87 after lost 3.7; from 1345 to 1402 it is 328 with nothing lost and 329 with 6.2. A mean rate or share of the DMA engines does not say whether the next tile is there.
- I charged "20 tiles with 0.8" alone. Where I saw the engines "just full", at chunks 3 to 9 in the main groups (1222 to 1345), 0.1 us is lost. It is lost ahead of them, at the tiles with which chunks 3 to 9 are begun early, a term that I put at "nothing, or 4.8" and left out of the sum (3.8), and behind them, at chunks 10 to 12.
- I counted on "a lead of 8.2 us", the split buffers. That lead covers a late VectorE. Here the tile itself is late too (36.0 us of waits for DMA), and then there is nothing to split.

I had the number that spoke for it, a demand of "1.04: just full", and took it as small since 0.04 of 76 us is 3.0. But the engines were not full in the two stretches of the changed kernel that lose most, 0.87 and 0.89: bursts and pauses lie under the mean, and what makes the tiles late there is not in a sum of demands. The Trainium skill, "DMA: Bandwidth & Descriptors", section "Where 436 GB/s comes from", with some 358 GB/s as a core's share of HBM, had put the squeeze nearer its upper bound. The runs agree with that direction. They do not show that figure as a limit: the slices of 373 and 378 GB/s, by which I set the page aside, are means over 45 us, and the first FFN's down projection took 345 GB/s over 181 us before the change with 0.1 us lost.

**The first FFN** (0, bounds -3.2 and +3.2): right on the whole. 1.5 us less are lost up to 546 and 2.2 more behind it, and the old finish gives no other time.

**The rivals.** All hidden fell. "The squeeze not covered" named the right place, but its price, 7.6, was too low. The temporaries fell: no wait for a kept copy beyond the first pair shows in the changed kernel. "I am wrong in kind if the loss lies before 1100" did not come about; I was wrong in size, on the dearest term.

**What stays open.** Shown: the loss needs the rows' bytes (rows_short_load), comes with the new shares and early chunks (rates_alone) and hardly with the early chunks at 0.62 rows a tile (four_pairs_mix), and is not the time of VectorE's sums or the bookkeeping. Not settled: how much of it is the engines' rate and how much the pauses that transposes and rows make in SyncE's one queue. Neither does it alone: the half load lost 5.0 us up to 1222 at 256 GB/s, and most of the pauses, from 1222 to 1345, come with 0.1 lost. Each edit also lets the planner order the lists anew, and the first pair alone costs from 0.4 us (turns_later) to 4.9 (rows_short_load); a difference of a few us between two runs need not be the edit's own. Every version with fewer pairs gave back what it saved, and none beat the kernel before.
